# Scores of 64-wide heads in the two row halves of TensorE, in a float32 kernel of two transformer blocks

## The chip, the cores and the metric

The kernel runs on one core of a Trainium2 chip. The metric is the device time of one execution in microseconds (us), the median over runs; smaller is better. A core has TensorE (PE: matmuls and transposes on a 128x128 array, into PSUM banks), VectorE (DVE), ScalarE (ACT) and GpSimd (POOL), and DMA queues.

## The reference

A batch of one, 256 tokens `x` and 256 context tokens of 1024 features, float32, two blocks of two layers. Each layer of the first block normalises both streams and feeds three branches (a gated linear recurrence, differential attention, a Fourier mix), whose outputs are merged. Differential attention has 8 heads with two maps of 64 features:

```python
def attend(q, k, v, lam):
    s = jnp.einsum('bhmqd,bhmkd->bhmqk', q, k, preferred_element_type=jnp.float32) * (B_QK ** -0.5)
    p = jax.nn.softmax(s, axis=-1)
    w = p[:, :, 0] - lam * p[:, :, 1]
    return jnp.einsum('bhqk,bhkv->bhqv', w.astype(v.dtype), v)
```

In layer 0 the 256 context queries see the 256 context keys and the 256 `x` queries all 512 keys; in layer 1 only the `x` queries are needed. The second block's layer 0 has a mixer with 8 heads of dense attention and 8 heads of window attention with a sink, all of 64 features, four query heads to a key head (`mixer_ab`). Its layer 1 has 8 heads of latent attention (96 features) and 8 heads of neighbourhood attention (64 features, a bias by relative position) (`mixer_cd`). After each mixer come cross attention to a memory (4 heads of 128) and a gated feed-forward part.

## The kernel before

All products are float32 by pairs of float32r: `split` (L263) writes a high part with ACT (L267) and the rest with DVE (L268), and `mm3` (L256) multiplies high by high, high by low and low by high, three matmuls (L259, L260, L261) into one PSUM bank. Weights are split by `split_into`, the low part on DVE or POOL (L254). Instructions are put in order by a scheduler that fills gaps on each engine: matmuls of different parts of the program stand between each other on PE.

Scores of heads of 64 features would use half of the array's rows. `stack_q` (L273) and `stack_k` (L279) fill all 128: a stacked query has its high part in rows 0 to 63 and its low part in rows 64 to 127, a key has its high part twice (two ACT copies, L282 and L283), and a second key tile has the low part over zeros that stay there (`zeroed`, filled once by `make_zeroed`). `mm_stacked` (L298) then needs two matmuls (L300, L301) instead of three. This is used in three places:

- `b_stage1` (L1110) and `b_head` (L1141), branch b: for each pair of heads keys and queries are normalised, rotated, transposed (L1138) and stacked by head and map. For each head, stream and query tile of 128 tokens, the two maps get a PSUM bank of scores each (tag `sc`, two banks), maximum (L1161), exponential (L1162), and the weighted difference is transposed (L1169), split and multiplied with the values.
- `mixer_ab` (L1375): a unit is a pair of heads of one kind, eight units. For each of two query tiles both heads' scores go into one `sc` bank, `softmax_t` (L1283) works on the two heads at once, and the window's mask comes in by a matmul with the identity (L1450).
- `near_project` (L1463) and the neighbourhood part of `mixer_cd` (L1482), with the scores in an `mm` bank.

`pair_values` (L1321) multiplies the transposed weights with two heads' values: the even head with 64 stationary columns, the odd one with 128 (its own last), into two halves of a `pv` bank, and each head's 64 rows are split apart. `softmax_t` is also used by `cross` (L1602) with `mm3` scores. The second block's pool has 16 `act`, 8 `q`, 4 `p`, 3 `e` tiles; PSUM has banks mm 3, sc 2, tp 2, pv 1.

Of the kernel before, what the change touches and what calls it, by code (L numbers as in the profile page):

```python
# [6 lines left out]
F32 = mybir.dt.float32  # L7
F32R = mybir.dt.float32r
# [7 lines left out]
P = 128  # L16
# [20 lines left out]
SOFTMAX = dict(ab=(0, 1), cd=(1, 1), x=(1, 0))  # L37
# [41 lines left out]
def _constants():  # L79
# [51 lines left out]
    # Tokens t and 256 - t come folded, their sums with the cosines and their differences with  # L131
    # the sines; row 0 has the sum and the difference of tokens 0 and 128.
# [59 lines left out]
# ----------------------------------------------------------------------------  # L192


def interleave(*parts):
    """Emits the steps of several generators in turn."""
    parts = list(parts)
    while parts:
        parts = [p for p in parts if next(p, parts) is not parts]


class Build:
# [5 lines left out]
    def share(self, part):  # L208
        """Lets GpSimd take every nth of the weights' splits from here on."""
# [10 lines left out]
    def u(self, tag, shape=None, dt=F32):  # L220
        """A tile of up to UNIT words in the working pool."""
# [26 lines left out]
    def split_into(self, h, lo, raw):  # L248
        """The float32r pair of weights; GpSimd takes its share of the low parts."""
# [6 lines left out]
    def mm3(self, out, a, b, start, stop):  # L256
        """out += a[0]+a[1] transposed, times b[0]+b[1], but for the product of the low parts."""
# [5 lines left out]
    def split(self, h, lo, src, scale=None):  # L263
        """src (float32, SBUF or PSUM), times a column if given, into a float32r pair."""
# [8 lines left out]
    def stack_q(self, out, src):  # L273
        """out [128, n]: the high part of src [64, n] over its low part."""
        nc = self.nc
        nc.scalar.copy(out[:64], src)
        nc.vector.tensor_tensor(out[64:], src, out[:64].bitcast(F32), op=ALU.subtract)

    def stack_k(self, out, src):  # L279
        """Pair [128, n]: the high part of src [64, n] twice; its low part over the zeros that out[1] has."""  # L280
        nc = self.nc
        nc.scalar.copy(out[0][:64], src)  # L282
        nc.scalar.copy(out[0][64:], src)  # L283
# [1484 lines left out]
```

## Time and profile before

| | us |
|---|---|
| median of 3 runs | 2494.37 |
| the runs | 2493.41, 2494.37, 2500.68 |
| span of the profiled execution (first to last instruction) | 2498.4 |
| PE, DVE, ACT, POOL busy in it | 2323.3, 1705.2, 1214.7, 715.6 |

The profile is of one execution; its own time is not given beside the span. "Busy" is the time in which an engine executes; weight loads (PEld) overlap matmuls. The mean granted clock of PE over the span is 0.967 of full speed. An entry "idle before <- X" says how long an engine stood idle before instructions of a group and whose result ended most of that. Matmuls are pipelined, so that the length of one (0.40 us for 512 columns) is longer than the distance between the starts of two.

### The profile page before, as it was taken

The page shows a single profiled execution, that of the slowest core. Times are in us where ns is not written, and L with a number is a line of the kernel's source. Part 1 is how long each engine was busy: PE and PEld are TensorE (multiplying, and loading weights), DVE is VectorE, ACT ScalarE, POOL GpSimd, SP SyncE. Part 2 cuts the span into 40 slices and gives each one's busy share as a digit, 9 for nine tenths or more (in the row PEclk, how much of TensorE's full clock was granted, in tenths as well). Part 3 has the DMA queues.
Part 4 walks back from the last instruction along what each step waited for, and adds up shares of the span by engine and source line. Part 5 has one row for each costly group of instructions (what it writes and reads, how often), then busy time and mean ns, then how long its engine had stood idle before and what let it go on. Part 6 is the DMA issues. An engine that isn't in the chain of part 4 may idle for free.

```text
span 2498.4 us, 40872 instructions
## 1 busy us (share of the span) xinstructions
PE 2323.3 (93%) x15610; PEld 2093.4 (84%) x15610; DVE 1705.2 (68%) x3469; ACT 1214.7 (49%) x2260; POOL 715.6 (29%) x456
## 2 busy tenths in 40 slices
PE   5899999999999999989999988998688999988998
PEld 3688879888897787879989988898578999778998
DVE  8645657477676545586676767766887765887765
ACT  5244444456546233335555544644465544675443
POOL 4242321122222112043134534423343221222221
PEclk8899999999999999999999989999899999999999
DMA  6122234333323434433445322455223555433554
GB/s 245 51 85 94 94 116 144 122 106 110 113 95 115 163 109 148 146 114 123 131 156 168 120 89 89 155 186 193 85 85 121 184 182 190 133 103 126 183 183 141
DMA packets 111076, 330.90 MB, mean 132 GB/s; under 512 B 12320, under 2 KB 24352, under 8 KB 110880
## 3 DMA queue, kind: packets, MB, share of 16 engines
q1 hardware_dynamic: 90432, 299.87, 36.4%
q10 hardware_dynamic: 20448, 28.42, 3.4%
q8 instruction: 123, 2.02, 0.3%
q14 instruction: 73, 0.60, 0.1%
HBM read 309.36 MB, written 18.87 MB: 131 GB/s over the span
## 4 chain that ended last, share of the span: by engine, by line
PE 36%; DVE 14%; ACT 3%; issue 2%; DMA 1%; POOL 0%; ACTq 0%; DVEq 0%; POOLq 0%
PE mm L259 10%; PE mm L260 10%; PE mm L261 10%; DVE h L271 1%; DVE w_low L254 1%; DVE e L1308 1%; ACT w_high L253 1%; PE pv L259 1%; DVE mx L1288 1%; PE pv L260 1%; PE pv L261 1%; PE tp L1310 0%; ACT e L1295 0%; DVE b_rs_t L335 0%; DMA load<-yacc 0%
## 5 line engine op out<-in xcount | busy, mean ns | idle before, releaser
L253 ACT CAST w_high<-w_raw 128x1024 fp32r<-128x1024 f32 (+1 forms) x522 | 540.4, 1039 | 589.3 <-PE mm L260 342.1
L254 POOL TENSOR_TENSOR w_low<-w_raw,w_high 128x1024 fp32r<-128x1024 f32 x181 | 442.5, 2452 | 856.1 <-ACT w_high L253 704.3
L259 PE MATMUL mm<-big,w_high 128*128 128x512 f32 (+1 forms) x1664 | 575.8, 348 | 21.9 <-DVE v L268 7.2
L260 PE MATMUL mm<-big,w_high 128*128 128x512 f32 (+1 forms) x1664 | 575.0, 346 | 0.0
L261 PE MATMUL mm<-big,w_low 128*128 128x512 f32 (+1 forms) x1664 | 573.0, 346 | 1.1 <-DVE w_low L254 0.8
L254 DVE TENSOR_TENSOR w_low<-w_raw,w_high 128x1024 fp32r<-128x1024 f32 (+1 forms) x341 | 424.9, 1247 | 161.3 <-ACT w_high L253 157.8
L259 PEld LDWEIGHTS mm<-big,w_high 128*128 128x128 f32 x1664 | 318.9, 192 | 66.8 <-issue 15.1
L261 PEld LDWEIGHTS mm<-big,w_low 128*128 128x128 f32 x1664 | 318.3, 192 | 39.7 <-DVE w_low L254 1.3
L260 PEld LDWEIGHTS mm<-big,w_high 128*128 128x128 f32 x1664 | 319.4, 192 | 37.1 <-DVE big L268 0.4
L260 PE MATMUL mm<-w_low,big 128*128 128x256 f32 x960 | 271.8, 285 | 2.5 <-POOL w_low L254 2.5
L259 PE MATMUL mm<-w_high,big 128*128 128x256 f32 x960 | 268.7, 285 | 4.7 <-DVE q L268 4.7
L261 PE MATMUL mm<-w_high,big 128*128 128x256 f32 x960 | 270.6, 284 | 0.0
L260 PE MATMUL mm<-h,w_high 128*128 128x256 f32 x896 | 255.1, 285 | 4.9 <-DVE h L271 4.1
L259 PE MATMUL mm<-h,w_high 128*128 128x256 f32 x896 | 253.5, 284 | 2.7 <-ACT h L270 1.7
L261 PE MATMUL mm<-h,w_low 128*128 128x256 f32 x896 | 253.7, 283 | 0.0
L260 PEld LDWEIGHTS mm<-w_low,big 128*128 128x128 f32 x960 | 184.1, 192 | 5.4 <-POOL w_low L254 4.3
L259 PEld LDWEIGHTS mm<-w_high,big 128*128 128x128 f32 x960 | 182.4, 192 | 7.0 <-DVE q L268 4.9
L261 PEld LDWEIGHTS mm<-w_high,big 128*128 128x128 f32 x960 | 183.9, 192 | 0.6
L260 PEld LDWEIGHTS mm<-h,w_high 128*128 128x128 f32 x896 | 169.6, 189 | 7.9 <-DVE h L271 7.8
L259 PEld LDWEIGHTS mm<-h,w_high 128*128 128x128 f32 x896 | 169.4, 189 | 4.4 <-ACT h L270 2.8
L261 PEld LDWEIGHTS mm<-h,w_low 128*128 128x128 f32 x896 | 169.7, 190 | 0.1
L1658 POOL TENSOR_TENSOR x<-x,r 128x256 f32<-128x256 f32 x44 | 60.3, 1371 | 190.7 <-ACT t L1657 190.7
(481 smaller groups left out, 4656.3 us busy)
## 6 DMA issues: line engine op xcount, KB each, us to landing
w_raw<-wstream SPq DMA_DIRECT2D x486, 512.0 KB, 3.3
w_raw<-wstream SPq DMA_DIRECT2D x32, 448.0 KB, 3.1
big<-wstream SPq DMA_DIRECT2D x16, 512.0 KB, 5.8
gates<-y ACTq DMA_DIRECT2D x24, 256.0 KB, 2.0
w<-gates SPq DMA_DIRECT2D x18, 256.0 KB, 3.9
load<-yacc ACTq DMA_DIRECT2D x16, 256.0 KB, 3.8
yacc<-w ACTq DMA_DIRECT2D x12, 256.0 KB, 2.1
gates<-y ACTq DMA_DIRECT2D x24, 128.0 KB, 2.9
```

The costliest lines, as they stand in the source:

```text
L253: nc.scalar.copy(h, raw)
L254: eng.tensor_tensor(lo, raw, h.bitcast(F32), op=ALU.subtract)
L259: nc.tensor.matmul(out, a[0], b[0], start=start, stop=False)
L260: nc.tensor.matmul(out, a[0], b[1], start=False, stop=False)
L261: nc.tensor.matmul(out, a[1], b[0], start=False, stop=stop)
L271: nc.vector.scalar_tensor_tensor(lo, src, scale, h.bitcast(F32), op0=ALU.mult, op1=ALU.subtract)
L1288: nc.vector.reduce_max(mx, ps2, axis=AX.X, negate=True)
L1308: nc.vector.tensor_scalar(p[:, u], p[:, u], sm[:, u:u + 1], None, op0=ALU.mult)
L1658: nc.gpsimd.tensor_tensor(g, g, rb, op=ALU.mult)
```

## The change

`stack_q`, `stack_k`, `zeroed`, `make_zeroed` and `mm_stacked` go. Queries and keys of two heads (or of a head's two maps) lie in the partitions 0 to 63 and 64 to 127 of one float32r pair, as the transposition leaves them, and are split once. `halves` multiplies them with the three products of `mm3` for each head, in the upper or lower 64 rows of the array, each head into its own PSUM bank. `softmax_t` takes both query tiles of two heads at once, by head. In `mixer_ab` the keys are rotated into both halves (`twice`), and the values lie between zero columns (`padded`), so that both heads' products add up in one bank and are split once. The bias of the neighbourhood comes by head instead of by query tile. Comments were taken out, which shifts line numbers (L278 is the matmul in `halves`).

```diff
-SECOND = dict(load=2, act=16, q=8, p=4, x=4, e=3, s=2, t=3, r=2)
+SECOND = dict(load=2, act=14, vz=4, q=8, p=4, x=4, e=3, s=2, t=3, r=2)
...
-    def mm_stacked(self, out, q, k, start=True, stop=True):
-        nc = self.nc
-        nc.tensor.matmul(out, q, k[0], start=start, stop=False)
-        nc.tensor.matmul(out, q, k[1], start=False, stop=stop)
+    def halves(self, outs, a, b, start=True, stop=True):
+
+        for i, (x, y) in enumerate(((0, 0), (0, 1), (1, 0))):
+            for u in range(2):
+                r = slice(64 * u, 64 * u + 64)
+                self.nc.tensor.matmul(outs[u], a[x][r], b[y][r], start=start and i == 0, stop=stop and i == 2)
...
             pt = self.b_transposed(kr, u, 0)
-            for m in range(2):
-                k = self.u("k", dt=F32R), self.zeroed()
-                self.stack_k(k, pt[64 * m:64 * m + 64])
-                ks.append(k)
+            ks.append((self.u("k", dt=F32R), self.u("k", dt=F32R)))
+            self.split(*ks[u], pt)
             pt = self.b_transposed(qr, u, self.q0)
-            for m in range(2):
-                q = self.u("q", dt=F32R)
-                self.stack_q(q[:, self.t0:], pt[64 * m:64 * m + 64, self.t0:])
-                qs.append(q)
+            qs.append((self.u("q", dt=F32R), self.u("q", dt=F32R)))
+            self.split(*(x[:, self.t0:] for x in qs[u]), pt[:, self.t0:])
...
-                for m in range(2):
-                    ps = self.bank("sc")[:, :nk * P]
-                    self.mm_stacked(ps, qs[m][:, qsl], tuple(x[:, :nk * P] for x in ks[m]))
+                pss = [self.bank("sc")[:, :nk * P] for _ in range(2)]
+                self.halves(pss, [x[:, qsl] for x in qs], [x[:, :nk * P] for x in ks])
+                for m, ps in enumerate(pss):
                     nc.vector.reduce_max(mx[:, m:m + 1], ps, axis=AX.X, negate=True)
...
-    def softmax_t(self, ps2, pts, qi, sink=None, row_scale=None):
+    def softmax_t(self, srcs, pts, sink=None, row_scale=None):
...
+        mx, sm = self.small("mx", [P, 2, 2]), self.small("sm", [P, 2, 2])
+        for u in range(2):
+            nc.vector.reduce_max(mx[:, u], srcs[u], axis=AX.X, negate=True)
...
+        p = [self.u("e").rearrange("p (t c) -> p t c", t=2) for _ in range(2)]
         for u in range(2):
+            for t in range(2):
+                nc.scalar.activation(p[u][:, t], srcs[u][:, t], AF.Exp, bias=mx[:, u, t:t + 1], scale=1.0 if row_scale is None else row_scale[:, t:t + 1],
+                                     accum_out=sm[:, u, t:t + 1])
...
         nc.vector.reciprocal(sm, sm)
...
+            self.split(pts[0][:, u], pts[1][:, u], pt.rearrange("p s t c -> p s (t c)"))
...
+    def padded(self, n):
+
+        v = tuple(self.u("vz", [P, 64 * (2 * n + 1)], F32R) for _ in range(2))
+        for x in v:
+            self.nc.gpsimd.memset(x[:, :P * n].rearrange("p (g c) -> p g c", c=P)[:, :, :64].bitcast(F32), 0.0)
+            self.nc.gpsimd.memset(x[:, P * n:].bitcast(F32), 0.0)
+        return v, tuple(x[:, 64:].rearrange("p (g c) -> p g c", c=P)[:, :, :64] for x in v)
+
+    def pair_values(self, y, k, pts, vs, zeros=False):
+
+        if zeros:
+            po = self.bank("pv")[:, :S]
+            for u in range(2):
+                for s in range(2):
+                    self.mm3(po, vs(u, s), (pts[0][:, u, s], pts[1][:, u, s]), u == 0 and s == 0, u == 1 and s == 1)
+            self.split(y[0][:, k, :S], y[1][:, k, :S], po)
+            return
...
+                pss = [self.bank("sc") for _ in range(2)]
+                if kind == 1:
+                    for u in range(2):
+                        nc.tensor.matmul(pss[u], eye, win, start=True, stop=False)
                 for qi in range(2):
...
+                    self.halves([x[:, qi * S:(qi + 1) * S] for x in pss], [x[:, qsl] for x in qT[kind][pr // 2]], [x[:, ksl] for x in kT[kind]], kind == 0, kind == 0 or qi == 1)
+                self.softmax_t([x.rearrange("p (t c) -> p t c", t=2) for x in pss], pts, sink=[x[:, 2 * pr:2 * pr + 2] for x in sink] if kind else None)
...
-                bias = self.u("load", [P, UNIT])[:, :512]
-                nc.sync.dma_start(bias, self.io["rpb"][pr, qi])
...
-            a = self.u("act" if f < 16 else "q", [P, 2, S], F32R)
+            a = self.u("act" if f < 14 else "q", [P, 2, S], F32R)
```

The program writes the six matmuls of `halves` in turn, upper, lower, upper, lower. The scheduler then puts them in an order of its own. Three places of the built programs show it.

First, PE in layer 0 of branch b, first head, the context's stream, first query tile. Here `mm` is the bank of another projection, `sc` the scores, `k` and `q` keys and queries, `kz` a key tile over zeros. Before:

```order
L261 MATMUL mm_4287<-big_791,w_low_4284 128x512
L300 MATMUL sc_4325<-k_3993,q_4006 128x256
L301 MATMUL sc_4325<-kz_76,q_4006 128x256
L300 MATMUL sc_4330<-k_3997,q_4009 128x256
L301 MATMUL sc_4330<-kz_78,q_4009 128x256
L259 MATMUL mm_4449<-big_210,w_high_4445 128x512
```

With the change:

```order
L261 MATMUL mm_4267<-big_783,w_low_4264 128x512
L278 MATMUL sc_4305<-k_3985,q_3994 128x256
L278 MATMUL sc_4306<-k_3985,q_3994 128x256
L278 MATMUL sc_4305<-k_3986,q_3994 128x256
L278 MATMUL sc_4306<-k_3986,q_3994 128x256
L278 MATMUL sc_4305<-k_3985,q_3995 128x256
L278 MATMUL sc_4306<-k_3985,q_3995 128x256
L259 MATMUL mm_4437<-big_202,w_high_4433 128x512
```

Four matmuls of 128 rows became six of 64, here in turn (4305 is the upper half, 4306 the lower).

Second, the same head, the stream of `x`, second query tile. With the change:

```order
L260 MATMUL mm_4544<-big_203,w_high_4540 128x512
L278 MATMUL sc_4394<-k_3985,q_3994 128x512
L278 MATMUL sc_4394<-k_3986,q_3994 128x512
L278 MATMUL sc_4394<-k_3985,q_3995 128x512
L261 MATMUL mm_4544<-big_202,w_low_4541 128x512
L278 MATMUL sc_4395<-k_3985,q_3994 128x512
L278 MATMUL sc_4395<-k_3986,q_3994 128x512
L259 MATMUL pv_4298<-w_4299,v_3923 128x256
L278 MATMUL sc_4395<-k_3985,q_3995 128x512
L260 MATMUL pv_4298<-w_4300,v_3923 128x256
```

Three matmuls of the upper half now stand together, then the lower half's, and matmuls of 128 rows (a projection's, the values') stand between them.

Third, ACT in stage 1 of branch b, the same pair of heads, with `tp` the transposed keys and `w_high` the weights' high parts. Before:

```order
L282 CAST k_3993<-tp_3988 64x512
L283 CAST k_3993<-tp_3988 64x512
L282 CAST k_3997<-tp_3988 64x512
L283 CAST k_3997<-tp_3988 64x512
L253 CAST w_high_4143<-w_raw_4141 128x1024
```

With the change:

```order
L267 CAST k_3985<-tp_3980 128x512
L253 CAST w_high_4123<-w_raw_4121 128x1024
L974 DMA yacc_598<-w_4047 128x512
L971 DMA load_8386<-yacc_598 128x512
L253 CAST w_high_4158<-w_raw_4156 128x1024
```

One copy of 128 partitions stands where four of 64 stood, and the weights' copy follows it at once.

Counted over the whole of PE's order: a visit is a stretch of 64-row matmuls between matmuls of 128 rows, and a step is one 64-row matmul, or two neighbours of different halves, or before one matmul of 128 rows.

| stage | score matmuls before, now | visits now | steps of 256 columns before, now | steps of 512 columns before, now |
|---|---|---|---|---|
| branch b, layer 0 | 128, 192 | 53 | 64, 66 | 64, 87 |
| branch b, layer 1 | 64, 96 | 32 | | 64, 81 |
| `mixer_ab` | 64, 96 | 27 | 64, 85 | |
| `mixer_cd`, neighbourhood | 32, 48 | 6 | 32, 46 | |

Over the whole program PE's order has 14990 rows before and 15130 with the change, DVE's 3326 and 3228, ACT's 2168 and 2045, POOL's 462 and 462, SP's 614 and 614.

## Rows read from the trace of the kernel before

**Rows 1.** The page: its heading, and busy time, share and instructions of each engine.

```profile
span 2498.4 us, 40872 instructions
...
PE 2323.3 (93%) x15610; PEld 2093.4 (84%) x15610; DVE 1705.2 (68%) x3469; ACT 1214.7 (49%) x2260; POOL 715.6 (29%) x456
```

**Rows 2.** Windows by stage: us, then busy (x) of PE, PEld, DVE, ACT, POOL; clock, DMA.

```profile
560.00:880.00 320.00, 317.41 (x1826) 269.79 (x1825) 208.05 (x471) 164.28 (x308) 74.91 (x34) 0.99 0.36 121
1380.00:1560.00 180.00, 156.28 (x1203) 153.13 (x1202) 128.62 (x285) 88.20 (x163) 82.85 (x37) 0.92 0.30 97
1720.00:1800.00 80.00, 56.24 (x235) 44.88 (x234) 61.20 (x133) 34.91 (x64) 35.34 (x18) 0.83 0.35 121
1800.00:1860.00 60.00, 49.75 (x325) 42.56 (x325) 54.20 (x132) 39.42 (x113) 18.69 (x9) 0.94 0.19 62
...
2125.00:2245.00 120.00, 105.33 (x725) 93.67 (x725) 96.42 (x200) 80.65 (x194) 28.85 (x19) 0.96 0.36 117
```

**Rows 3.** Timeline of PE near 205 us: start us, length us, instruction.

```profile
204.76 0.40 PE L260 MATMUL mm<-big,w_high 128*128 128x512 f32 x1
204.99 0.40 PE L261 MATMUL mm<-big,w_low 128*128 128x512 f32 x1
205.32 1.13 PE L885 MATMUL sc<-negm,ident 4*128 4x512 f32 x4
206.38 0.50 PE L259 MATMUL mm<-big,w_high 128*128 128x512 f32 x1
206.71 0.39 PE L260 MATMUL mm<-big,w_high 128*128 128x512 f32 x1
```

**Rows 4.** Timeline of PE near 138 us.

```profile
138.25 1.12 PE L885 MATMUL sc<-negm,ident 4*128 4x512 f32 x2
139.30 0.50 PE L259 MATMUL mm<-big,w_high 128*128 128x512 f32 x1
```

**Rows 5.** Timeline of PE near 1172 us.

```profile
1172.22 0.28 PE L260 MATMUL mm<-big,w_high 128*128 128x256 f32 x1
1172.34 0.28 PE L261 MATMUL mm<-big,w_low 128*128 128x256 f32 x1
1172.55 0.69 PE L885 MATMUL sc<-negm,ident 4*128 4x256 f32 x2
1173.17 0.39 PE L259 MATMUL mm<-big,w_high 128*128 128x256 f32 x1
1173.40 0.28 PE L260 MATMUL mm<-big,w_high 128*128 128x256 f32 x1
```

**Rows 6.** Groups by line and form, whole span, DVE and ACT: busy us, mean ns, idle before.

```profile
L284 DVE TENSOR_TENSOR kz<-tp,k 64x512 fp32r<-64x512 f32 x32 | 22.0, 687 | 19.6 <-ACT k L283 19.4
...
L268 DVE TENSOR_TENSOR p<-tp,p 128x512 fp32r<-128x512 f32 x32 | 21.6, 685 | 4.0 <-ACT p L267 3.8
...
L282 ACT CAST k<-tp 64x512 fp32r<-64x512 f32 x32 | 18.6, 581 | 22.4 <-PE tp L1138 17.9 <-DVE kz L284 3.6 <-ACT y L981 0.4
...
L267 ACT CAST p<-tp 128x512 fp32r<-128x512 f32 x32 | 18.5, 582 | 14.1 <-PE tp L1310 13.7
```

**Rows 7.** Groups by line and form on DVE, 1795 to 1860 us (the units of l = 0).

```profile
L268 DVE TENSOR_TENSOR y<-pv,y 64x256 fp32r<-64x256 f32 x15 | 6.3, 421 | 3.5 <-ACT y L267 3.2
L277 DVE TENSOR_TENSOR q<-tp,q 64x512 fp32r<-64x512 f32 x5 | 3.5, 691 | 0.3 <-ACT q L276 0.2
L1299 DVE TENSOR_TENSOR sink<-vecs,mx 128x2 f32<-128x2 f32 x8 | 2.8, 361 | 0.0
L1302 DVE RECIPROCAL sm<-sm 128x2 f32<-128x2 f32 x16 | 2.4, 156 | 0.3 <-ACT e L1295 0.2
```

**Rows 8.** The chain of waits, 1380 to 1570 us: start us, us, what.

```profile
1416.78 0.23 PE sc L301
...
1473.46 2.33 DVE b_rs_t L334
```

More of the change, by code (lines that the diff above doesn't have):

```diff
@@ L1143, in b_head @@
         t0, tn = self.t0, self.tn
-        qs, ks = (x[2 * (hd % 2):2 * (hd % 2) + 2] for x in st[:2])
+        qs, ks = (x[hd % 2] for x in st[:2])
         vp = st[2]
@@ L1326, in pair_values, with rope_tok @@
             for s in range(2):
-                vh, vl = vs(u, s)
-                self.mm3(po[:m, u], (vh, vl), (pts[0][:, u, s], pts[1][:, u, s]), s == 0, s == 1)
+                self.mm3(po[:m, u], vs(u, s), (pts[0][:, u, s], pts[1][:, u, s]), s == 0, s == 1)
             rows = slice(64 * u, 64 * u + 64)
             self.split(y[0][rows, k, :S], y[1][rows, k, :S], po[rows, u])
-    def rope_tok(self, out, x, c, s, n, half):
+    def rope_tok(self, out, x, c, s, n, half, twice=False):
         nc = self.nc
@@ L1342, in rope_tok @@
         t = t.rearrange("p n b c -> p n (b c)")
+        if twice:
+            o, t = (v.unsqueeze(2).broadcast_to([P, n, 2, 2 * half]) for v in (o, t))
         out = out if isinstance(out, list) else [out]
@@ L1387, in mixer_ab @@
             nc.scalar.activation(kx, pss[t][:, :256], AF.Copy, scale=r[:, t:t + 1])
-            v = tuple(self.u("act", dt=F32R) for _ in range(2))
-            vsrc = pss[t][:, 256:].rearrange("p (g c) -> p g c", c=64)
-            for dup in range(2):
-                o = [x.rearrange("p (g u c) -> p g u c", u=2, c=64)[:, :, dup] for x in v]
-                self.split(o[0], o[1], vsrc, scale=r[:, t:t + 1])
+            v, at = self.padded(4)
+            self.split(*at, pss[t][:, 256:].rearrange("p (g c) -> p g c", c=64), scale=r[:, t:t + 1])
             vv.append(v)
@@ L1396, in mixer_ab @@
             self.head_norm(ka, 2, self.vec("g_ka"))
[L1397 to L1400 removed]
+            kr = self.u("x")
+            kv = kr.rearrange("p (g u c) -> p g u c", u=2, c=64)
+            self.rope_tok(kv[:, 0:2], ka, tab["r2_c"][:, t], tab["r2_s"][:, t], 2, 32, twice=True)
+            self.rope_tok(kv[:, 2:4], kb, tab["r1_c"][:, t], tab["r1_s"][:, t], 2, 32, twice=True)
             for g in range(4):
[L1403 removed]
+                nc.tensor.transpose((kt_ps, kt_ps2)[g // 2][:, (g % 2) * S + t * P:(g % 2) * S + (t + 1) * P], kr[:, P * g:P * g + P], self.ident)
         kT = []
         for src in (kt_ps, kt_ps2):
[L1406 to L1408 removed]
+            kT.append(tuple(self.u("act", dt=F32R) for _ in range(2)))
+            self.split(*kT[-1], src)
         y = self.new_y2()
@@ L1438, in mixer_ab @@
                 qT[kind].append([self.u("q", dt=F32R) for _ in range(2)])
-                for u in range(2):
-                    self.stack_q(qT[kind][i][u], ptq[i][64 * u:64 * u + 64])
+                self.split(*qT[kind][i], ptq[i])
         for pr in range(4):
@@ L1470, in near_project @@
             self.nc.vector.tensor_tensor(t, ps, rb, op=ALU.mult)
-            for u in range(2):
-                if j == 0:
-                    q = self.u("q", dt=F32R)[:, :S]
-                    self.stack_q(q, t[64 * u:64 * u + 64])
-                    qk.append(q)
-                else:
-                    k = self.u("q", dt=F32R)[:, :S], self.zeroed()[:, :S]
-                    self.stack_k(k, t[64 * u:64 * u + 64])
-                    qk.append(k)
+            qk.append(tuple(self.u("q", dt=F32R)[:, :S] for _ in range(2)))
+            self.split(*qk[j], t)
         return qk
@@ L1574, in mixer_cd @@
             pts = self.new_pts()
-            for qi in range(2):
-                ps = self.bank("sc").rearrange("p (u c) -> p u c", u=2)
-                for u in range(2):
-                    a, b = pair[u]
+            pss = [self.bank("sc").rearrange("p (t c) -> p t c", t=2) for _ in range(2)]
+            for u in range(2):
+                a, b = pair[u]
+                for qi in range(2):
                     qsl = slice(qi * P, (qi + 1) * P)
-                    self.mm3(ps[:, u], (a[:, 0, qsl], b[:, 0, qsl]), (a[:, 1], b[:, 1]), True, True)
-                self.softmax_t(ps, pts, qi)
+                    self.mm3(pss[u][:, qi], (a[:, 0, qsl], b[:, 0, qsl]), (a[:, 1], b[:, 1]), True, True)
@@ L1582, in mixer_cd @@
+            self.softmax_t(pss, pts)
             self.pair_values(y, pr, pts, lambda u, s, pr=pr: tuple(x[:, P * pr:P * pr + 64 * (u + 1)] for x in vc[s]))
             pts = self.new_pts()
+            pss = [self.bank("sc") for _ in range(2)]
             for qi in range(2):
+                self.halves([x[:, qi * S:(qi + 1) * S] for x in pss], [x[:, qi * P:(qi + 1) * P] for x in qk[0]], qk[1])
+            srcs = []
+            for u in range(2):
                 s2 = self.u("s")
                 bias = self.u("load", [P, UNIT])[:, :512]
-                nc.sync.dma_start(bias, self.io["rpb"][pr, qi])
```

109 lines of the change are left out of this document (31 added, 78 removed).

## Prediction

> **What bounds the kernel now.** I read the page first. TensorE (PE) is busy for 2323.3 of 2498.4 us, 93%, VectorE (DVE) for 68%, ScalarE (ACT) for 49% [rows 1]. That share is an average, so I next read the stages that the change touches, in windows [rows 2]. Five matter. From 560 to 880 us branch b of the first layer runs: PE is busy for 317.4 of 320 us, so whatever PE gains or loses there lands in full. From 1380 to 1560 us the same branch runs in the second layer with half the tokens: PE 156.3 of 180, DVE 128.6. There the chain passes between engines. It holds score matmuls (0.23 us at 1416.78) and the small steps of a norm on DVE, one of them 2.33 us long [rows 8]. From 1720 to 1800 us the second block's first layer projects its queries and keys (DVE 61.2 of 80, PE 56.2), and from 1800 to 1860 its eight units of scores, softmax and values run with DVE at 54.2 of 60 and PE at 49.8. From 2125 to 2245 us (mixer_cd) PE has 105.3 of 120 and DVE 96.4.
>
> **What PE has to do, new against old.** The order shows 432 score matmuls in place of 288, in 118 visits: stretches in which the array is split in two and before and after which it works whole. Two prices decide, that of a step and that of a visit.
>
> A step. Ordinary matmuls begin 0.23 us apart with 512 columns [rows 3] and 0.12 us apart with 256 [rows 5]. I take the same for a matmul of 64 rows, because the columns are what streams, and take two neighbours of different halves as one step. The nearest row for that is line 885, the only one that uses a part of the array's rows, 4 of them: four such matmuls, of two directions in two row groups, go from 205.32 to 206.38 [rows 3], and two of one direction from 138.25 to 139.30 [rows 4], so the second direction was free. Beside those rows stands a rule of the Trainium skill, page "TensorEngine Tiling (Array Packing)", section "Overview": a contraction of at most 64 can run up to twice as fast in two row tiles. By it the six matmuls of two heads would cost three steps where before they cost four, and all stages together would lose 12 us of PE time. The sum goes by the order instead, which the rule does not speak of: where the program wrote the halves in turn, the scheduler put three or six of one half in a row, and matmuls of one half follow each other. Counted so, the steps rise by 2 of 256 columns and 23 of 512 in layer 0 of branch b, by 17 of 512 in layer 1, by 21 of 256 in mixer_ab and by 14 of 256 in mixer_cd. That is 5.5 + 3.9 + 2.5 + 1.7 = 13.6 us.
>
> A visit. Around line 885 PE loses time that no column explains. From the last whole matmul's start to the start of the second after the visit it takes 204.99 to 206.71, 1.72 us [rows 3]; two ordinary steps are 0.46 of it, so the visit takes 1.26. With 256 columns it is 1172.34 to 1173.40, 1.06, less 0.24, so 0.82 [rows 5]. The columns halve, so 0.44 is the price of half the columns and 0.82 - 0.44 = 0.38 us is left whatever the columns. One sees it lie on both sides: the first L885 starts 0.33 us after its neighbour's start, where 0.23 is usual, and the second whole matmul starts 0.33 us after the first [rows 3]. I take 0.38 us for a visit of 64 rows too. Its ends are 0, were the split in halves free where the split by 32 rows is not, and 0.38. Visits: 53 in layer 0 of branch b (20.1 us), 32 in layer 1 (12.2), 27 in mixer_ab (10.3), 6 in mixer_cd (2.3), together 44.9 us. PE's added time is then 25.6, 16.1, 12.8 and 4.0 us by stage, 58.5 in all.
>
> **What the other engines lose.** A split costs by columns and not by partitions: ACT takes 581 ns for 64x512 and 582 for 128x512, DVE 687 and 685 [rows 6]. For each pair of heads in branch b, ACT had eight copies for the keys (each high part twice) and four for the queries and now has two and two; DVE had four and four and has two and two. In layer 0 that is 8 x 0.58 = 4.6 us of ACT and 4 x 0.69 = 2.8 of DVE a pair. All of it lies beside PE there, which is idle for 2.6 us of 320, so it returns 2 at most. In layer 1, where PE waits 23.7 of 180 us, some lies on the chain.
>
> In the units of mixer_ab, DVE loses half of 16 reciprocals, half of the sink additions and minima, and half of the two output splits of a unit: 2.4/2 + 2.8/2 + about 1.4 for the smaller ones, 6.3/2 = 3.2 for y, and 2.8 of q's splits that lie in this window [rows 7], 10 us together. The products with zero columns are as many as before, 12 a unit, of 128 columns instead of 64 and 128; a matmul's time goes by the streamed columns, so they cost nothing. GpSimd's eight zero fills replace eight; POOL is busy for 18.7 of 60 us there. In mixer_cd and the cross attention the coarser softmax saves about 5 and 1 us of DVE by the same rows. Sixteen `act` tiles become fourteen: if a split of mixer_cd waits for one, it and its successor are late, 2 x (0.58 + 0.69) = 2.5 us [rows 6]; if the scheduler's order hides it, 0. I take 1. The bias tiles are as many DMAs of the same size, laid out by head, where the DMA engines are busy for 0.36 of the time [rows 2]: nothing.
>
> **The sum, stage by stage.** Branch b, layer 0: +25.6, less 2 of idle time: +24. Layer 1: PE is busy for 87% of it, so 14 of the 16.1 land, and of the relief one copy and one subtraction a pair, 4 x 1.3 = 5, were ahead of the scores: +9. mixer_ab's projections: four of eight splits of keys and queries go in a stretch that DVE limits: -2. Its units: DVE falls from 54 to 44 but PE rises from 49.8 to 62.6 in a stretch of 60, so PE becomes the bound: +3. mixer_cd: +4.0 + 1 against 5 of DVE that is about as busy as PE, and half of PE's own idle time goes: -2. Cross: 0. The sum is +32 us. The profiled span of 2498.4 us (the profile gives no other time of that execution) would become 2530; the median of the three runs shown, 2494.4, lies 4 us under the span, so I put the change on the median: 2494.4 + 32 = 2526 us, a little over 1% slower.
>
> **Rivals.**
>
> A, the other side: the visit is free. It has one mechanism: a switch between whole array and 64-row halves overlaps with the matmul before, as the weight loads of ordinary matmuls do (PEld 2093.4 us beside PE's 2323.3 in one span [rows 1]). Then the steps alone count: layer 0 +5.5 - 2 = +3.5, layer 1 +3.9 - 7 = -3, mixer_ab -8 (DVE's 54 become 44, PE's 49.8 become 52.3, and PE sets the end), mixer_cd -3: 2484 us. For it: line 885 is float32 of 4 rows and not float32r of 64, so its gap may have another cause. Against it: the gap does not depend on columns and lies on both sides of the visit. It decides from a visit under about 0.08 us (10 of 118). By the Trainium skill's rule above, with three steps for six matmuls and free visits, it would be some 20 us less still; no run shows that here.
>
> B, half price: a visit costs 0.19 us, since with two loads of weights ahead in the other half one of the two gaps closes. PE's sum falls by 22.4; of that the stages pass on 10 + 5 + 5 + 1 = 21: 2505 us.
>
> C, nothing is absorbed: the chain in layer 1 and the units keeps its waits, and all 58.5 us land: 2553. For it: PE sets the end in most stages. Against it: PE's idle 23.7 us in layer 1.
>
> D, the change does not do what it says: halves do not run side by side at 64 rows. Then 432 matmuls stand in a row, 144 more (32 of each size in layer 0, 32 of 512 in layer 1, 32 and 16 of 256 after), that is 64 x 0.23 + 80 x 0.12 = 24 us instead of 13.6: 2536.
>
> E, the coarser softmax: a unit now holds both score banks and two of three `e` tiles until both query tiles are read, so the next unit's scores start later. If each of 20 units (8, 8 and 4) waits for one exponential and one scaling more, about 0.7 + 0.7 us as the 512-column rows have it, 28 us come on top: 2554.
>
> **Chances.** Forecast (2515 to 2536) 0.34; A 0.19; B 0.22; C 0.10; D 0.08; E 0.07. A measurement of this kernel can tell about 0.3% from no change, 7.5 us: 2487 to 2502. Of A 0.16 is faster and 0.03 the same, of B 0.09 is the same and 0.13 slower; the rest is slower: faster 0.16, same 0.12, slower 0.72. The range reaches from A's time to C's, 2484 to 2553; outside lie half of A, half of E and the edge of C. Without A, the slower cases alone lie between 2503 and 2553.
>
> **What would show it.** In the profile of the changed kernel, the start of the first L278 of a visit comes 0.1 us late, and so does the second whole matmul after it; two L278 of different halves start at the same time and two of one half 0.12 or 0.23 us apart. Layer 0 of branch b is about 24 us longer at a PE that is still never idle, mixer_ab's units have DVE at about 44 us and are not shorter. I am wrong if L278 follows its neighbour at the ordinary distance (A), if layer 0 is longer by 14 or less (B), or if two halves never start together (D); and in E the idle time ahead of the first L278 of a unit names a reader of the score bank.

## The result: 0.7% slower

The changed kernel takes 2513.89 us (median of 4 runs, 2512.52 to 2515.50) against 2493.89 us for the kernel before (2492.22 to 2500.68): 20.0 us more, a ratio of 1.0071 (95% interval 1.0058 to 1.0083). The forecast was 2526, with a range from 2484 to 2553 and a chance of 0.72 for slower. The direction and the range held; of the 32 us that were forecast, 20 came.

The page of the changed kernel, heading and busy times, answers to [rows 1]:

```profile
span 2512.4 us, 40954 instructions
...
PE 2360.9 (94%) x15754; PEld 2094.5 (83%) x15754; DVE 1649.1 (66%) x3371; ACT 1165.2 (46%) x2152; POOL 708.9 (28%) x456
```

PE is busy for 37.6 us longer and the span grew by 14.0; DVE and ACT lost 56 and 50 us of work. The time of an execution is 1.8 to 2.1 us over its span in the other traces; by that the profiled execution of before took some 2500 us, 6 over the median of its runs. So the traces differ by 14 us where the medians differ by 20, and a difference of one or two us between stages is not read here.

To compare stage by stage I cut both traces at the same weight split (L253 on ACT occurs in the same order in both). The windows of the kernel before (start:end, length, then busy us of PE, PEld, DVE, ACT, POOL with their instructions, granted clock, DMA share and GB/s) are branch b of layer 0 with the end of its neighbours, the stretch to branch b of layer 1, that branch with the start of branch c, mixer_ab with its cross attention, and mixer_cd with its own:

```profile
455.30:902.70 447.40, 443.58 (x2593) 379.38 (x2592) 284.75 (x641) 224.20 (x423) 103.24 (x47) 1.00 0.36 119
902.70:1324.00 421.30, 401.89 (x2579) 357.14 (x2578) 286.05 (x592) 182.47 (x340) 106.62 (x82) 0.98 0.40 130
1324.00:1661.10 337.10, 303.50 (x2387) 295.80 (x2386) 234.67 (x498) 177.06 (x330) 146.22 (x69) 0.96 0.42 137
1661.10:1947.10 286.00, 243.01 (x1645) 219.38 (x1644) 223.41 (x441) 151.62 (x319) 102.47 (x60) 0.93 0.37 123
2131.50:2346.10 214.60, 193.08 (x1420) 178.55 (x1419) 169.37 (x322) 132.91 (x292) 54.66 (x40) 0.96 0.39 130
```

The same windows of the changed kernel:

```profile
453.30:927.90 474.60, 467.85 (x2658) 382.50 (x2657) 271.34 (x630) 210.51 (x400) 101.14 (x47) 0.99 0.34 112
927.90:1352.50 424.60, 402.24 (x2580) 356.86 (x2578) 287.36 (x592) 182.36 (x339) 106.62 (x82) 0.98 0.41 129
1352.50:1681.50 329.00, 311.50 (x2419) 292.59 (x2418) 215.78 (x482) 160.05 (x297) 144.74 (x69) 0.98 0.44 141
1681.50:1963.90 282.40, 249.95 (x1677) 221.87 (x1677) 207.32 (x399) 143.51 (x294) 101.81 (x64) 0.95 0.38 124
2148.30:2359.90 211.60, 193.65 (x1436) 179.24 (x1435) 162.46 (x299) 126.94 (x272) 54.09 (x40) 0.97 0.41 132
```

| stage | forecast | traces |
|---|---|---|
| branch b, layer 0 | +24 | +27.2 |
| to branch b, layer 1 | 0 | +3.3 |
| branch b, layer 1 | +9 | -8.1 |
| mixer_ab and cross attention | +1 | -3.6 |
| mixer_cd and cross attention | -2 | -3.0 |

Layer 0 pays what was forecast. Layer 1 was forecast to lose 9 us and gained 8: PE's busy time there rose by 8.0 us, yet the stage became shorter, because PE idled for 17.5 us where it had idled for 33.6 (length less busy time).

How a visit looks, on the timeline of PE in the changed kernel (start, length, instruction; neighbours of one form are joined, x6 are six). First with the halves in turn:

```profile
471.10 0.40 PE L259 MATMUL mm<-big,w_high 128*128 128x512 f32 x1
471.33 0.40 PE L260 MATMUL mm<-big,w_high 128*128 128x512 f32 x1
471.66 0.97 PE L278 MATMUL sc<-k,q 64*128 64x512 f32 x6
472.56 0.50 PE L261 MATMUL mm<-big,w_low 128*128 128x512 f32 x1
472.89 0.40 PE L259 MATMUL mm<-big,w_high 128*128 128x512 f32 x1
```

Then with three of one half, the others after them:

```profile
478.23 0.40 PE L260 MATMUL mm<-big,w_high 128*128 128x512 f32 x1
478.56 0.96 PE L278 MATMUL sc<-k,q 64*128 64x512 f32 x3
479.45 0.50 PE L261 MATMUL mm<-big,w_low 128*128 128x512 f32 x1
479.88 0.73 PE L278 MATMUL sc<-k,q 64*128 64x512 f32 x2
480.54 0.38 PE L259 MATMUL pv<-w,v 128*128 128x256 f32 x1
480.85 0.50 PE L278 MATMUL sc<-k,q 64*128 64x512 f32 x1
481.28 0.38 PE L260 MATMUL pv<-w,v 128*128 128x256 f32 x1
```

Six matmuls in turn take 0.97 us and three of one half 0.96: the halves do run side by side, as [rows 3, 4] had it for 4 rows. And the visit starts 0.33 us after its neighbour's start, where 0.23 is usual, and the second whole matmul behind it starts 0.33 us after the first (472.56 to 472.89): the same gaps as at line 885. By the single records the three steps of the visit start at 471.66, 472.00 and 472.23, the two halves of each within 0.01 us, and take 0.90 us instead of 0.70. So this visit costs 0.10 + 0.20 + 0.10 = 0.40 us, and a step inside it keeps the ordinary 0.23. In the second place the three matmuls of the lower half came in two visits more.

Fewer than 128 rows do not bring such a gap by themselves. The latent heads' scores use 96 rows, and in the kernel before they stand between whole matmuls, at the ordinary distance of 0.12 us for 256 columns on both sides:

```profile
2164.47 0.28 PE L261 MATMUL mm<-h,w_low 128*128 128x256 f32 x1
2164.59 0.28 PE L260 MATMUL sc<-q,q 96*128 96x256 f32 x1
...
2165.20 0.28 PE L259 MATMUL sc<-q 96*128 96x256 f32 x1
2165.32 0.28 PE L259 MATMUL mm<-h,w_high 128*128 128x256 f32 x1
```

### The profile page after: what moved, and what is told of

Read it like the earlier page. It is cut to its first block, busy times and chain, and to the rows that moved or that the text cites. A ratio compares the mean times of both kernels' runs of the same rounds, so it can differ in the third digit from the quotient of the medians.

```text
span 2512.4 us, 40954 instructions
## 1 busy us (share of the span) xinstructions
PE 2360.9 (94%) x15754; PEld 2094.5 (83%) x15754; DVE 1649.1 (66%) x3371; ACT 1165.2 (46%) x2152; POOL 708.9 (28%) x456
## 5 line engine op out<-in xcount | busy, mean ns | idle before, releaser
L253 ACT CAST w_high<-w_raw 128x1024 fp32r<-128x1024 f32 (+1 forms) x522 | 540.6, 1039 | 639.1 <-PE mm L260 375.8
L260 PE MATMUL mm<-w_low,big 128*128 128x256 f32 x960 | 272.3, 285 | 1.4 <-POOL w_low L254 1.4
```

Source lines behind the costliest of these rows:

```text
L253: nc.scalar.copy(h, raw)
L260: nc.tensor.matmul(out, a[0], b[1], start=False, stop=False)
```

## The experiments

The theory of the loss: each switch of the array between 128 rows and halves costs about 0.4 us, and the order makes 118 visits. Its rivals: the 64-row matmuls themselves cost the time, or the new softmax and the waits for score banks do. For layer 1's gain there were two theories: fewer copies and subtractions ahead of the scores (theory 1), or an order in which small DVE steps meet GpSimd's weight splits less often (theory 2).

**No switching (whole_rows).** The change, with all 128 rows in each score matmul. Each score then adds up both heads' products, so this kernel leaves the separate scores out; it serves only to time the engines' work.

```diff
-                r = slice(64 * u, 64 * u + 64)
-                self.nc.tensor.matmul(outs[u], a[x][r], b[y][r], start=start and i == 0, stop=stop and i == 2)
+                self.nc.tensor.matmul(outs[u], a[x], b[y], start=start and i == 0, stop=stop and i == 2)
```

> The change as it is, but each of the six score matmuls uses all 128 rows of the array, so that PE never switches; the scores then add up both heads' products (that part of the computation is changed). Steps become 432 in a row: by 0.12 and 0.23 us a step 72.6 us where the order of the change gives 62.0, so +10.6 on PE; 118 visits of 0.40 us go, -47. Theory (the switch is what costs): layer 0 of branch b about 16 us shorter than with the change (53 visits less, 5.6 us of steps more), the whole about 2484 (2478 to 2492), and no 0.33 us distance around the score matmuls. Rival 1 (a 64-row matmul or the finer splitting of work costs, not the switch): no shorter than the change, 2514 to 2525. Rival 2 (the time is in the softmax and the waits for score banks): 2510 to 2516.

Measured: 2494.50 us, ratio to before 0.9996 (0.9982 to 1.0010). Some 19 us of the change's 20 went with the switches, although 144 matmuls more stand in a row than in the kernel before. On PE's timeline, at the same pair's scores as at 471.66 above:

```profile
467.75 1.53 PE L277 MATMUL sc<-k,q 128*128 128x512 f32 x6
469.12 0.39 PE L261 MATMUL mm<-big,w_low 128*128 128x512 f32 x1
469.35 0.39 PE L259 MATMUL mm<-big,w_high 128*128 128x512 f32 x1
```

Six steps of 0.23 us, 1.37 from 467.75 to 469.12, and 0.23 to the next. So the switch is what costs, and both rivals fall: the new softmax is still in this kernel, and a 64-row matmul inside a visit takes the ordinary 0.23 us (472.00 to 472.23 above). The gain in layer 0 was 9.2 us, not 16. The stages of layer 0, layer 1 and mixer_ab in this kernel:

```profile
449.60:915.00 465.40, 458.12 (x2658) 392.53 (x2657) 273.29 (x630) 210.79 (x400) 101.52 (x47) 0.99 0.35 114
1340.70:1664.70 324.00, 304.51 (x2419) 297.60 (x2418) 216.34 (x482) 159.40 (x298) 144.33 (x69) 0.97 0.45 143
1664.70:1940.80 276.10, 241.86 (x1677) 219.90 (x1676) 202.66 (x399) 143.11 (x295) 101.45 (x64) 0.96 0.39 127
```

That the whole takes the time of the kernel before is a sum of two things. Layer 0 is still 18.0 us longer than before, 11.2 of them for 64 matmuls more in a row, while layer 1 and mixer_ab are 13.1 and 9.9 us shorter.

For the size I summed, over all PE instructions of layer 0's stage, the distance from one start to the next less the ordinary distance of that width. Around and within the 53 visits the change has 16.9 us of this, and 3.5 us more than the kernel before elsewhere (the second whole matmul after a visit, above all): 20.4 us, 0.38 a visit. With whole rows 3.4 of these stay, so the switch itself is 17.0 us, 0.32 a visit. What stays fits the clock: in layer 0 TensorE was granted the lower of its two levels (0.5 in these rows, 1.2 of 2.4 GHz) for 10.2 us with the change, for 13.7 with whole rows and for 3.4 before. With the change it was so from 513.6 and from 865.2 us, after PE had waited 3.5 and 1.5 us for `diag`; 6.8 us more at half speed than before are 3.4 us:

```profile
513.60:517.00 3.40, 3.40 (x16) 2.95 (x13) 1.25 (x3) 2.09 (x5) 2.17 (x1) 0.51 0.46 143
865.20:872.00 6.80, 5.37 (x16) 4.09 (x16) 4.42 (x13) 2.88 (x4) 0.47 (x1) 0.50 0.00 0
```

**The two blocks apart (halves_b, second_only).** The first has the change's `b_stage1` and `b_head` in the kernel before; the second has the changed kernel with `b_stage1`, `b_head` and the stacked scores of before.

```diff
-        qs, ks = (x[2 * (hd % 2):2 * (hd % 2) + 2] for x in st[:2])
+        qs, ks = (x[hd % 2] for x in st[:2])
...
-                    self.mm_stacked(ps, qs[m][:, qsl], tuple(x[:, :nk * P] for x in ks[m]))
+                self.halves(pss, [x[:, qsl] for x in qs], [x[:, :nk * P] for x in ks])
```

> The kernel before with the change in branch b of the first block alone; the second block as before. Theory (layer 0 of branch b costs 27 us, layer 1 gives back 7 to 10, and the blocks do not act on each other): 2494 + 20 to 26 = 2514 to 2520, the first block's stages as in the change. Rival (the stages of the second block are what gives the time back and branch b's layer 1 gains nothing when seen alone): 2521 to 2530.

> The change in the second block alone, branch b with stacked scores as before. Theory (DVE-limited units gain more from fewer splits and sink steps than 33 visits cost): 2494 - 5 to - 9 = 2485 to 2489. Rival (the gains seen in mixer_ab and mixer_cd belong to what branch b did earlier, a shift of loads): 2494 or more. Together with the branch-b kernel the two differences should add up to the change's +20.

Measured: branch b alone 2522.20 us, 1.0114 (1.0099 to 1.0130), 28 us over its kernel before; the second block alone 2488.91, 0.9982 (0.9970 to 0.9994), 5 us under. The two add up to 22, the change's 20 within the intervals. The branch-b kernel was slower by more than the 20 to 26 that were expected, and its time lies in the rival's range. But the rival's reason, no gain in layer 1 of branch b alone, is not what the traces show. Layer 1's stage in the branch-b kernel, then in the other one, whose first block is that of before:

```profile
1354.20:1684.50 330.30, 311.06 (x2419) 291.35 (x2418) 216.28 (x482) 159.88 (x298) 144.86 (x69) 0.98 0.44 140
1322.80:1659.80 337.00, 300.46 (x2387) 292.44 (x2386) 236.47 (x498) 177.08 (x329) 146.81 (x69) 0.97 0.43 137
```

These repeat the 329.0 and 337.1 us of the two kernels themselves; layer 0 takes 476.0 and 447.5. The second block gains although it makes 33 visits.

**The written order kept (pinned).** PE must issue the six matmuls in turn, and they come ahead where they are ready.

```diff
-        for i, (x, y) in enumerate(((0, 0), (0, 1), (1, 0))):
+        with self.tc.manual_schedule(engines={mybir.EngineType.PE}), self.tc.high_priority():
+            for i, (x, y) in enumerate(((0, 0), (0, 1), (1, 0))):
...
```

> The change, with PE held to the written order in the six score matmuls (upper, lower, upper, lower) and these moved ahead where they are ready. By the order the steps fall from 62.0 to 45.0 us and the visits from 118 to 111. Theory (two halves in turn run side by side, a visit costs 0.40): PE loses 17 + 3 = 20 us less than with the change, of which 12 to 20 reach the end: 2494 to 2502. Rival (keeping two banks' scores together makes PE wait for the later bank): idle time ahead of score matmuls of 0.3 us or more a group, 2510 to 2520.

Measured: 2521.96 us, 1.0110 (1.0091 to 1.0129), so 8 us slower than the change. A miss, beyond the rival's range too. Layer 0 of branch b did gain, 463.4 us against 474.6. But branch b's layer 1 rose from 329.0 to 336.1, PE's idle time in it from 17.5 to 24.0, and mixer_cd's stage from 211.6 to 220.0. The idle time is not where the rival had it. In layer 1 no listed wait of PE is ahead of a score matmul of branch b; new are 4.3 us ahead of a transposition and 2.3 ahead of the values. In mixer_cd the waits ahead of scores are 3.7 us where they were 2.2. That scores which come early hold up what stood between them is a guess, and the order and the priority were not tried apart.

**The copies put back (redundant).** The change, with keys' and queries' splits of branch b repeated.

```diff
-            self.split(*ks[u], pt)
+            for _ in range(4):
+                nc.scalar.copy(ks[u][0], pt)
+            for _ in range(2):
+                nc.vector.tensor_tensor(ks[u][1], pt, ks[u][0].bitcast(F32), op=ALU.subtract)
...
```

> The change with the copies and subtractions of keys and queries in branch b repeated until ACT and DVE have as many as before (a head: four copies and two subtractions for its keys, two and two for its queries); the results stay the same. Theory 1 (layer 1 of branch b gained because ACT and DVE had less to do ahead of the scores): PE's idle time there goes from 11.7 us back to 20 to 26, layer 1 is 7 to 14 us longer than with the change, layer 0 0 to 2, the whole 2522 to 2530 where the change had 2514. Theory 2 (layer 1 gained because the order moved small DVE steps away from GpSimd's weight splits): idle stays at 8 to 14 us, the whole 2512 to 2518.

Measured: 2520.28 us, 1.0099 (1.0083 to 1.0114), 6 us above the change. Layer 0 did not move (474.9); layer 1's stage went from 329.0 to 336.3 and PE's idle time there from 17.5 to 23.0. Of the 8 us that the change gained there, 7 go when the copies come back, as theory 1 says; the whole lies between what the two theories gave, so by its time this run does not decide. But the waits of PE there show how. The kernel with copies (line that waited, what for, total us, times, longest):

```profile
PE mm L259 <- DVE b_rs_y L313: 7.1, 1, 7.1
PE tp L333 <- DVE diag L332: 4.8, 3, 2.5
PE pv L260 <- DVE w L268: 4.1, 2, 2.9
```

The change without them (the 11.7 us that the expectation calls idle time equal this wait; all of PE's idle time in the stage is 17.5):

```profile
PE tp L333 <- DVE diag L332: 11.7, 4, 5.7
```

The kernel before, in the same stage:

```profile
PE tp L356 <- DVE diag L355: 10.7, 5, 3.2
PE mm L259 <- DVE v L268: 6.8, 1, 6.8
PE mm L259 <- DVE b_rs_t L334: 5.0, 1, 5.0
PE mm L260 <- POOL w_low L254: 0.4, 1, 0.4
```

What the copies bring back is not many small delays of 0.6 us, but above all one wait of 7.1 us for a norm's step (the tiles `b_rs_*` are the steps of its Newton iteration, `diag` is made from their result).

**GpSimd's share (pool2_before, pool2_after, pool0_before).** Why a norm's step is late is seen on DVE's timeline in the kernel before, at the 6.8 us wait:

```profile
1473.46 2.32 DVE L334 SCALAR_TENSOR_TENSOR b_rs_t<-b_rs_y 128x2 f32<-128x2 f32 x1
1475.81 2.27 DVE L335 TENSOR_TENSOR b_rs_t<-b_rs_t,b_rs_v 128x2 f32<-128x2 f32 x1
1478.11 2.26 DVE L336 SCALAR_TENSOR_TENSOR b_rs_y<-b_rs_t,b_rs_y 128x2 f32<-128x2 f32 x1
1480.30 0.68 DVE L1106 TENSOR_TENSOR h<-h,s 128x512 f32<-128x512 f32 x1
1480.90 0.15 DVE L334 SCALAR_TENSOR_TENSOR b_rs_t<-b_rs_y 128x2 f32<-128x2 f32 x1
```

and on POOL's at the same time:

```profile
1473.36 7.00 POOL L254 TENSOR_TENSOR w_low<-w_raw,w_high 128x1024 fp32r<-128x1024 f32 x3
```

Three steps on two columns, 0.15 us each when alone, take 2.3 us each, as long as one of GpSimd's three weight splits. They end at 1475.78, 1478.08 and 1480.38 us, the splits at 1475.76, 1478.07 and 1480.36. The values' split (`v`) for which PE waited comes behind them on DVE, at 1481.94. The Trainium skill, page "SBUF — State Buffer", section "SBUF: two separate sides", says that a DVE operation with two inputs in SBUF and a GpSimd operation that reads SBUF hold a pair of ports in turn, and that the later one blocks until the other's whole instruction is over. The rows agree.

Each trace has 104 DVE steps from two columns to two columns in layer 1's stage, with a median of 0.16 us. How many took over 1 us, and what all of them took beyond 0.16 us each:

| kernel | over 1 us | beyond 0.16 us each, together |
|---|---|---|
| before | 14 | 27.7 us |
| the change | 5 | 11.3 us |
| the change with the copies put back | 9 | 17.2 us |
| before, half of GpSimd's share (below) | 4 | 8.2 us |
| the change, half of the share | 5 | 9.3 us |
| before, no share | 1 | 1.2 us |

In the kernel before 75 of the 104 ran beside no instruction of GpSimd, and none of these took over 0.17 us.

The change pays for collisions elsewhere. The new wait of 3.5 us for `diag` in layer 0 stands behind one:

```profile
508.67 2.37 POOL L254 TENSOR_TENSOR w_low<-w_raw,w_high 128x1024 fp32r<-128x1024 f32 x1 [2.62 <-PE sc L278]
508.75 2.31 DVE L311 SCALAR_TENSOR_TENSOR b_rs_t<-b_rs_y 128x4 f32<-128x4 f32 x1
```

The next kernels give GpSimd every second low part in layer 1 of branch b, or none.

```diff
-POOL = dict(start=(2, 0), g0=(1, 0), g1=(1, 0), a0=(4, 1), a1=(0, 0), b0=(2, 1), b1=(1, 0), c0=(3, 0), c1=(3, 0),
+POOL = dict(start=(2, 0), g0=(1, 0), g1=(1, 0), a0=(4, 1), a1=(0, 0), b0=(2, 1), b1=(2, 1), c0=(3, 0), c1=(3, 0),
```

For none it is `b1=(0, 0)`.

> The kernel before, with GpSimd taking every second low part of the weights in layer 1 of branch b instead of every one. Theory 2 (PE's waits of 6.9 and 5.0 us there are DVE's small norm steps, stretched from 0.16 to 2.3 us while GpSimd splits weights): these two waits shrink to under 3 us each, and the kernel is 4 to 10 us faster than before, 2484 to 2490. Theory 1: DVE gets 18 more splits of 1.25 us, and the kernel is the same or up to 10 us slower.

> The change, with GpSimd taking every second low part of the weights in layer 1 of branch b. Theory 2 (the order let the change miss collisions that cost the kernel before 12 us): the change has little to gain, 2509 to 2516, and against the kernel before with the same share it is 24 to 32 us slower instead of 20. Theory 1 (fewer copies): the distance of the two stays at 16 to 23 us.

> The kernel before, with no weight split on GpSimd in layer 1 of branch b. Theory (collisions of GpSimd's splits with small DVE steps cost there, and DVE has room): no wait over 3 us for a norm's step, but 18 more splits of 1.25 us on DVE than with the half share, whose DVE was busy for 233 of 314 us: 2466 to 2476. Rival (DVE becomes the bound): 2480 to 2495, with PE waiting for low parts of weights.

Measured: the kernel before with half the share 2467.47 us, 0.9883 (0.9870 to 0.9897), with none 2465.18, 0.9876 (0.9860 to 0.9893). The first is 29 us faster, three times the most that was expected; the second is 32 faster, a little better than its 2466 to 2476. The change with half the share 2509.55, 1.0053 (1.0039 to 1.0067). With the share halved the change is not 20 but 42 us slower, where theory 2 gave 24 to 32 and theory 1 16 to 23. Layer 1's stage, before and then the change, each with half the share:

```profile
1317.40:1631.70 314.30, 298.28 (x2392) 290.44 (x2391) 235.25 (x529) 177.42 (x330) 85.50 (x43) 0.98 0.45 147
```

```profile
1348.60:1676.70 328.10, 313.48 (x2424) 293.50 (x2423) 229.27 (x513) 159.88 (x298) 84.69 (x43) 0.98 0.43 141
```

GpSimd's splits there fell from 54 to 28. 337.1 became 314.3 without the change and 329.0 became 328.1 with it. The collisions in the table fell by 19.5 us and by 2.0. Late weights are not the cause: PE waited only 0.4 us for a low part of GpSimd's in the kernel before (last of the waits above). The waits of 6.8 and 5.0 us are gone from the first, and `diag` is down to

```profile
PE tp L356 <- DVE diag L355: 2.6, 1, 2.6
```

where 10.7 stood. Without these waits the change costs 13.8 us in layer 1, not far from its 31 visits of 0.38 (11.8) and 4.9 us of more steps. With no share DVE has 56 instructions more in the stage than in the kernel before (234.67 us, x498) and is busy only 3.3 us longer:

```profile
1313.10:1628.80 315.70, 299.29 (x2391) 290.95 (x2391) 237.93 (x554) 177.96 (x330) 22.26 (x17) 0.98 0.46 147
```

Theory 2 holds in the main: the change gained in layer 1 by meeting GpSimd less often, 5 long steps instead of 14, though not never: its wait of 5.7 us for `diag` stands behind two of them. The copies of theory 1 count because they change whether a norm's steps meet GpSimd (9 instead of 5); that they cost something of their own too, as the 4.1 us for `w` may be, is not excluded.

**Stacked scores with the new softmax (stacked_second).** Branch b as before, the second block with the new softmax and padded values, but without halves; for room it has three zero tiles, `r` tiles of half the size and two `sink` tiles.

```diff
-                    self.halves([x[:, qi * S:(qi + 1) * S] for x in pss], [x[:, qsl] for x in qT[kind][pr // 2]], [x[:, ksl] for x in kT[kind]], kind == 0, kind == 0 or qi == 1)
+                    for u in range(2):
+                        self.mm_stacked(pss[u][:, qi * S:(qi + 1) * S], qT[kind][pr // 2][u][:, qsl], tuple(x[:, ksl] for x in kT[kind]), kind == 0, kind == 0 or qi == 1)
...
```

> Branch b as before; in the second block the new softmax and the values between zero columns, but the scores stacked as before, two matmuls of 128 rows each, without a visit. Against the second block of the change 33 visits of 0.40 us go (13 us) and the steps fall by 3.5; five to ten splits come back on DVE. Theory (visits cost, the rest of the change saves): 2494 - 12 to - 18 = 2476 to 2482, with mixer_ab's units shorter than in any kernel so far. Rival (the saving is the single split of two heads' queries and keys, not the softmax and the values): 2489 to 2494.

Measured: 2501.79 us, 1.0020 (1.0010 to 1.0030): slower than before, a miss beyond the rival too. mixer_ab with its cross attention takes 284.7 us, where it takes 278.3 in the kernel with the change in the second block alone (286.0 before). So that stage does not get shorter by doing without visits when the stacked splits come back; with these its DVE has 214.9 us of work instead of 206.3. Its trace is already 5.1 us late at the start of mixer_ab, where the program is still that of before; the profiled execution, 2505.97 us, is 4.2 over the median of its ten runs, and the rest of why is open. Whether the smaller pools cost something was not tried.

**The pieces that gain, together (best, best_ab).** The second block of the change, branch b stacked as before, GpSimd's share halved in layer 1 of branch b; `best_ab` halves it in mixer_ab too.

```diff
-            merge0=(0, 0), merge1=(0, 0), t=(4, 2), e=(1, 0), ab=(1, 0), x=(3, 2), cd=(3, 1), f=(0, 0))
+            merge0=(0, 0), merge1=(0, 0), t=(4, 2), e=(1, 0), ab=(2, 0), x=(3, 2), cd=(3, 1), f=(0, 0))
```

> Branch b with stacked scores as before, the second block as in the change, and GpSimd with every second low part of the weights in layer 1 of branch b. Theory (the pieces do not act on each other: -5 from the second block alone, -29 from GpSimd's share): 2494 - 34 = 2458 to 2464, with both verdicts faster. Rival (the second block's gain was a matter of the state that the first block left it in): 2466 to 2470, as with GpSimd's share alone.

> The same, with GpSimd taking every second low part in mixer_ab too. If DVE's small steps there are held up by GpSimd's weight splits as in layer 1 of branch b: 5 to 10 us less than the one before it. If DVE's own load sets the end in mixer_ab (DVE 54 of 60 us in the units before): 0 to 6 us more, since DVE gets a dozen splits of 1.25 us.

Measured: 2459.27 us, 0.9851 (0.9837 to 0.9866), and 2457.55, 0.9846 (0.9830 to 0.9861). Both beat both kernels, by 37 and 55 us or so. The first is 34 to 38 us under the kernel before, as the two pieces add up. In the second, mixer_ab's stage is 272.3 us against 282.9, but the times of the two cannot be told apart, so neither of the two expectations for it came.

## Why the prediction was right or wrong

- **The bound in layer 0** held: PE was idle for 3.8 us in that stage before and for 6.8 with the change, so PE's work is the time. Forecast were 20.1 us of visits, 5.5 of steps and 2 given back. The trace has 17.0 of visits, 3.5 of steps, 3.4 at the lower clock and 3.0 more of idle time: 26.9 of the 27.2. What failed is "it returns 2 at most": nothing was returned, and two waits for `diag` (5.0 us) are new, the longer of them behind a collision with GpSimd.
- **A visit of 0.38 us**, taken from matmuls of 4 rows, was right in kind: the same gaps stand on both sides of a visit. In size it was 0.32 on the average of layer 0's 53, by what whole rows save. That the sum around these visits gives 0.38 to the digit is luck, since it holds the lower clock. The prediction calls line 885 the only one that uses a part of the array's rows; the 96-row scores do too, and show no gap, so its 4 rows did not stand for every smaller height. Rivals A (free) and B (half) fall with the visit, C (nothing absorbed) with layer 1, and D with the six matmuls in 0.97 us.
- **Steps**: the count from the order was right in kind. They rose by 3.5 us in layer 0 and by 3.9 in layer 1 (forecast 5.5 and 3.9).
- **Layer 1** is the step that failed: "of the relief one copy and one subtraction a pair, 4 x 1.3 = 5, were ahead of the scores: +9". It was -8. I priced the stage by PE's busy share and took its waits as fixed. The row for the wait stood there, 2.33 us for a step on two columns [rows 8], and I read it as a slow norm and not as a collision with GpSimd that a new order would move. PE's idle time fell by 16.1 us; and the granted clock of the stage rose from 0.96 to 0.98, which gave back part of the visits' price. By the same sum as in layer 0 the 32 visits (12.2 us, 0.38 each) and the steps (3.9) cost what was forecast there, and the other matmuls took 7.0 us less.
- **Between the branches** +3.3 us came that no step named: two waits of 2.4 and 2.2 us in layer 1's first branch, in a new order. They stand in the traces of the change, of whole_rows and of halves_b, and in none with the old branch b; one of 1.8 us is gone. Why the order has them is open.
- **The second block** gained 5 us alone where -1 was forecast. DVE's work in mixer_ab's stage fell by 16.1 us. The projections take 76.2 us instead of 80.8 (forecast -2). The units and the cross attention, which overlap, take 162.4 instead of 161.7 (forecast +3): "PE becomes the bound" was wrong, since PE's idle time there, 19.6 us before and 12.6 now, took most of the visits up. mixer_cd's -3.0 stands beside a forecast of -2. Rival E did not show: PE's idle time ahead of L278 in the second block is 2.6 + 2.2 us in all groups together.
- **The sum**: forecast +32, measured +20. The direction rests on layer 0 alone, where PE sets the end; the largest error is layer 1 (17 us), and those of layer 0 and of the stretch behind it go the other way. That +20 came out so near to +32 is in part luck: with GpSimd's share halved the same change costs 42 us, 25.5 of them in layer 0 (474.4 against 448.9) and 13.8 in layer 1.

## What to carry over

Before packing two small contractions into the halves of the array, count from the built order how often PE leaves its full height and multiply by the price of a visit, here 0.3 to 0.4 us; only then count steps. A group of six in turn saves one step of four here, 0.23 us with 512 columns and 0.12 with 256. So, as an estimate from these rows, a visit has to hold two groups of 512 columns, or three to four of 256, before it pays. The order made 118 visits of 72 groups. Where a stage is not bound by PE, look at what its waits wait for: a two-column step of 2.3 us beside a GpSimd operation is a collision, and a change of order can move it, so that gains and losses there are not the edit's own. Remove such a wait first; here one number in a table was worth more than the whole change, in the other direction.

## What the runs showed of the hardware

- Leaving full height for halves of 64 rows and coming back costs 0.32 us a visit in layer 0 (17.0 us for 53) and 0.38 in layer 1 (12.2 for 32) between float32r matmuls, 0.40 in the visit shown; 96-row matmuls among whole ones cost nothing of the kind. What PE does in these gaps no run shows. Two halves in turn run fully side by side (0.97 us for six, 0.96 for three of one half).
- DVE operations on two columns go from 0.15 to 2.3 us while GpSimd splits weights. Halving GpSimd's share in layer 1 of branch b made that stage 23 us shorter (337.1 against 314.3) and the kernel 29; dropping it gives about the same (2467.5 and 2465.2 us).
- PE's mean granted clock in layer 1's stage was 0.96 with 33.6 us of idle time and 0.98 with 14.6 to 17.5, but it did not follow the idle time strictly: 0.97 with 36.5 in the kernel with the second block alone, 0.95 with 24.0 with the written order kept.
